# Parked sums of a down projection: added on VectorE at the second part's end, parked from GpSimd's queue, and brought back at spread times

## The chip, the cores and the metric

One core of a Trainium2 chip runs the whole layer in one launch. The time is that of the device for one execution, in microseconds; the median of several runs counts. TensorE (PE in the profile) multiplies matrices, VectorE (DVE) and ScalarE (ACT) work element by element, GpSimd (POOL) and SyncE (SP) issue DMAs here, each in the order of its own list of instructions.

## The reference

An encoder layer for 256 positions of width 2048, in float32. The part that matters here is the channel sub-layer, a gated feed-forward network of width 5632 between two normalisations, whose result is added to the residual stream; the sub-layer behind it needs that sum.

```python
h = h + rms_norm(mixed, g_mix_post[i])
fn = rms_norm(h, g_ffn_pre[i])
ff = (jax.nn.silu(fn @ w_ffn_gate[i]) * (fn @ w_ffn_up[i])) @ w_ffn_down[i]
h = h + rms_norm(ff, g_ffn_post[i])
gate = jax.nn.sigmoid(rms_norm(h, g_ple_pre[i]) @ w_ple_gate[i])
```

## The kernel before

**Products.** Every weight matrix comes from memory in tiles of 256 rows by 512 columns (512 KB, names `wr`, `third`, `lower`, `ple`). ScalarE casts a tile to a high part (`wh`, L624), VectorE takes the remainder (`wl`, L637), and PE does three products for each block (L671 to L673): a tile is 12 matmuls of 128x512. Some of the pairs of tiles in the feed-forward network are multiplied by a scheme with seven products instead of eight (L682 to L684); sums of weight blocks for it are made on VectorE (L572 to L582) and by accumulating DMAs of 256 KB from POOL's queue (L593). There are `W_BUFS = 4` pairs of buffers for split tiles and one more in the space of the gain vector (`w`, in the tile tagged `gain`).

**Stages.** The feed-forward width is worked off in three parts (`PARTS`, 4 + 4 + 3 groups of 512 columns). Each part first makes its columns of gate and up, turns the result (`mid`, moved to `mT` by sixteen small DMAs each) and then multiplies it by its rows of `w_ffn_down`, for four chunks of 512 output columns, two at a time. The chunks of parts 0 and 1 are only partial sums. `down_post` copies them on ScalarE from PSUM to a `mid` tile (L1802) and parks them in DRAM, `parts[0]` and `parts[1]`, from SP's queue (L1805, 512 KB each, eight in all). In part 2, `Sub.chunk` with `add=True` adds the last partial sum to the parked ones in the tiles `mg` (L1472), squares, multiplies by the gain, and the normalisation follows.

**What stands elsewhere meanwhile.** SBUF is short, so the tiles of `h` and `mg` (two of 1 MB each) hold other things during parts 0 to 2. `lower_tile` puts weight tiles of the seven-product scheme into the space of `h0` (slots 0 and 1) and of `mg0` (slots 3 and 4); slot 2 is in `ple`. `sums` lies in the space of `h1`, `s` in that of `mg1`. `h` itself is spilled to DRAM (`spill_h`). After the last product that reads those sums (`two_products`, `i == last_two`) everything comes back: `mg` plainly from `parts[0]` on SP's queue (L1827), then `parts[1]` onto it by accumulating DMAs of 1 MB from POOL's queue (`reload_sums`, `added`, L593), and `h` from its spill (`reload_h`, L1610). The gain vector comes by `next_gain` (L1424).

**Order.** A planner (`Plan`) in the program holds a clock for each engine and a list of generators, each of which says what it will do next, on which engine, at what cost and from when. It picks what can start first and so writes the order of each engine's instructions at build time. A due time given to `plan.add` only sets a place in that order; on the chip an instruction runs when its engine comes to it and its semaphores allow.

Of the kernel before, what the change touches and what calls it, by code (L numbers as in the profile page):

```python
# [10 lines left out]
F32 = mybir.dt.float32  # L11
F32R = mybir.dt.float32r
AF = mybir.ActivationFunctionType
ALU = mybir.AluOpType
AX = mybir.AxisListType

P = 128
S = 256
NT = S // P
D = 2048  # L20
# [7 lines left out]
N = 512  # L28
# [11 lines left out]
RING = 5  # L40
# [37 lines left out]
class Event:  # L78


    t = None
# [134 lines left out]
COST = {"act": 0.15, "dve": 0.08, "move": 150 / 340.0, "landing": 1.7}  # L216


def act(n, tables=COPY, take=None, give=None):
    return ("act", COST["act"] + 0.00082 * n, tables, take, give)  # L220


def dve(n, take=None, give=None):
    return ("dve", COST["dve"] + 0.00104 * n, None, take, give)
# [6 lines left out]
def dma(kb, take=None):  # L231
    return ("dma", kb / 340.0, None, take, None)
# [3 lines left out]
def layer(ctx: ExitStack, tc: tile.TileContext, a: dict, out: bass.AP):  # L236
    nc = tc.nc
# [4 lines left out]
    plan = Plan(wr=R_BUFS, w=W_BUFS, sm=SM_BUFS, acc=4, ev=1, mid=2, bt=2, m2=1, mt=1, sq=1, T0=1, T1=1, T4=1, **{f"{s}{j}": n for s, m, n in (("p", 5, 1), ("t", 3, 0)) for j in range(m)}, wr0=1, w0=1)  # L242

    def f32(t):
        return t.bitcast(F32)
# [11 lines left out]
    lower = {}  # L257
    more_w = {}

    def w_kind(i):  # L260
        return f"w{more_w[i]}" if i in more_w else "w"
# [16 lines left out]
    def raw_kind(i):  # L278
        if i in lower:
            return f"p{lower[i]}"  # L280
        return f"wr{more_raws[i]}" if i in more_raws else "wr"
# [85 lines left out]
    def done(event):  # L367
        event.t = plan.now
# [11 lines left out]
    class Act:  # L380


        def __init__(self, blocks=KD):
            self.at = {}
            self.ev = [Event() for _ in range(blocks)]
            self.sums, self.ev_sums = {}, {}
# [26 lines left out]
    tiles = []  # L413
    segs = []
# [92 lines left out]
    fours = {}  # L507
# [5 lines left out]
    ev_ple = Event()  # L513
# [3 lines left out]
    def pieces(i):  # L517

        return [slice(0, 1), slice(1, 2)] if i < EARLY else [slice(0, 2)]
# [71 lines left out]
    def added(dst, src, ev):  # L591
        yield ("pool", COST["move"], None, None, None)
        nc.gpsimd.dma_start(dst, src, accum_op=ALU.add)  # L593
        plan.now += ADDED
        done(ev)

    def last_sum(i):
        late, last, j, js, _, _ = fours[i]
        b = (3, 6, 7)[j]
        there = Event()  # L600
        yield from added(blocks()[:, b, :], late[:, 0, :], there)
        yield there
        if j == js[-1]:
            raws[last] = blocks()[:, 3:7:3, :] if len(js) == 2 else blocks()[:, 7:8, :]
            done(ev_raw[last, 2])
# [21 lines left out]
    def lo_stream():  # L627
        last_one = max(f[1] for f in fours.values())
        for i in range(len(tiles)):
            at_lo[0] = i  # L630
            for j in pieces(i):
                n = j.stop - j.start
                yield ev_hi[i, j.stop]
                src = raws[i] if n == 2 else raws[i][:, j, :]
                m = slice(j.start, j.start + src.shape[1])
                yield dve(src.shape[1] * N, give=gives.get(i) or raw_kind(i) if j.stop == 2 else None)
                nc.vector.tensor_tensor(  # L637
                    out=los[i][:, m, :], in0=src, in1=f32(his[i][:, m, :]), op=ALU.subtract
                )
                done(ev_lo[i, j.stop])  # L640
            raws.pop(i)
            if i == half_end:
                plan.add(reload_half(), plan.now + 76.0)
            if i in fours:
                plan.add(last_sum(i), plan.now, -2 * SOON)
            if i == last_one:
                done(ev_ple)

    MM = 0.216
    MM4 = 0.86  # L650
# [35 lines left out]
    def spent(i):  # L686
        his.pop(i), los.pop(i)
        at_pe[0] = max(at_pe[0], i)
        free_w(i)
        plan.run()  # L690

    def block(lhs, kx, t):
        return [x[:, t * P : (t + 1) * P] for x in lhs.at[kx]]
# [49 lines left out]
    def two_products(group, j, i):  # L743
        (C1, _, _), (C2, _, _) = group.chunks
        kx = group.sevens[j][1]
        s = group.lhs.sums[kx]
        plan.main(0, ev_lo[i, 2], group.lhs.ev[kx + 1], group.made)
        product(C1.accs[0], block(group.lhs, kx + 1, 0), i, 0, seeded=True)
        product(C2.accs[0], s["S4"], i, 1, seeded=True)
        spent(i)  # L750
        if i == last_two:
            for t in range(NT):
                plan.add(reload_sums(0, t), plan.clk["pe"] + 9.0 + 4.0 * t)
                plan.add(reload_sums(1, t), plan.clk["pe"] + 28.0 + 5.0 * t)
                plan.add(reload_h(t), plan.clk["pe"] + 50.0 + 12.0 * t)

    def one_product(group, js, i):
        (C1, _, _), _ = group.chunks
# [42 lines left out]
    def free_w(i):  # L801
        if i not in keep:
            plan.free[w_kind(i)].append(plan.clk["pe"])
        if i == max(more_w):
            plan.add(next_gain(("ffn", "g_ffn_post"), plan.clk["pe"] + 37.0), plan.clk["pe"] + 37.0)

    keep = set()
    def run_seg(s):
# [567 lines left out]
    for n, c in enumerate(ORDER.split()):  # L1376
        (n0, post), half = CHUNKS[c[0]], int(c[1])
        ch = Chunk(post(half), (open_p1, second_tiles)[n] if n < 2 else None)
# [10 lines left out]
    t2 = {}  # L1389

    class Halves:
        def __init__(self, pool, n):
            self.tiles = [
                pool.tile([P, D], F32, tag=f"{n}{t}", name=f"{n}{t}") for t in range(NT)
            ]

# [48 lines left out]
    ev_sums_back = Event()  # L1445
# [120 lines left out]
    def turn_h(c, hi, lo, nxt, gname):  # L1566
# [10 lines left out]
        for b in range(4):  # L1577
# [7 lines left out]
    spill = ctx.enter_context(  # L1585
        tc.tile_pool(name="spill", bufs=1, space=bass.MemoryType.DRAM)
    ).tile([NT, P, D], F32, name="h_spill")
    parts = [
        ctx.enter_context(
            tc.tile_pool(name=f"parts{i}", bufs=1, space=bass.MemoryType.DRAM)  # L1590
        ).tile([NT, P, D], F32, name=f"part{i}")
        for i in range(2)
    ]
    ev_spilled, ev_back = Event(), Event()
# [6 lines left out]
            nc.sync.dma_start(spill[t], t2["h"].tiles[t])  # L1601
        done(ev_spilled)

    halves_back = []

    def reload_h(t):
        if "back" not in t2:
            t2["back"] = Halves(t2["pool"], "h")
        yield dma(1024)
        nc.sync.dma_start(t2["back"].tiles[t], spill[t])  # L1610
        halves_back.append(t)
        if len(halves_back) == NT:
            t2["h"] = t2["back"]
            done(ev_back)

    half_spill = ctx.enter_context(
        tc.tile_pool(name="half_spill", bufs=1, space=bass.MemoryType.DRAM)
    ).tile([P, NT, D // 2], F32, name="ple_spill")
# [10 lines left out]
    def reload_half():  # L1629
        yield dma(1024)  # L1630
        nc.sync.dma_start(t2["ple"][:, :, 0 : D // 2], half_spill)
        done(ev_half_back)

    def next_gain(g, ready):
        yield from load_gain(g[1])
        done(ev_gain[g[0]])
# [32 lines left out]
    hF = Act()  # L1669
# [9 lines left out]
    def after_mix():  # L1679
# [5 lines left out]
    ch = [  # L1685
        Chunk(sub_post(mix, c, after=after_mix), None if c else open_p2,
              slot="sm" if c == 2 else "acc")
        for c in range(4)
    ]
# [10 lines left out]
    ffn = Sub("ffn", "g_ffn_post", "g_ple_pre")  # L1700
# [17 lines left out]
    def mid_tile():  # L1718
        return t2["pool"].tile([P, NT, N], F32, tag="mid", name="mid", bufs=2)
# [74 lines left out]

    def down_post(part, c):
        def post(ch):
            e = None
            for t in range(NT):
                yield act(N, take=None if t else "mid")
                if not t:  # L1800
                    e = mid_tile()
                nc.scalar.copy(e[:, t, :], ch.accs[t])  # L1802
            ch.release()
            yield dma(512)
            nc.sync.dma_start(  # L1805
                parts[part].rearrange("t p d -> p t d")[:, :, c * N : (c + 1) * N], e
            )
            plan.now += COST["landing"]
            plan.free["mid"].append(plan.now)
            ev_parts.append((part, c))  # L1810
        return post

    ev_parts = []

    def reload_sums(part, t):
        assert len(ev_parts) == 8
        if "mg_back" not in t2:
            t2["mg_back"] = t2["mg"] = Halves(t2["pool"], "mg")
        if part:
            there = Event()  # L1820
            yield from added(t2["mg"].tiles[t], parts[part][t], there)
            yield there
            if t == NT - 1:
                done(ev_sums_back)
        else:
            yield dma(1024)
            nc.sync.dma_start(t2["mg"].tiles[t], parts[0][t])  # L1827

    def after_ffn():
        return next_norm(ffn, hP, rstd_p, ev_rp, ("ple", "g_ple_post"))  # L1830
# [20 lines left out]
    for part, (f0, f1) in enumerate(PARTS):  # L1851
        mid = Mid(f"mid{part}")
        last_part = part == len(PARTS) - 1
        for f in range(f0, f1):
            slot = ring()
            g = Chunk(gate_post(f), slot=slot)
# [191 lines left out]
    n = 0  # L2048
# [6 lines left out]
        if i % (W_BUFS + MORE_W) < MORE_W:  # L2055
            more_w[i] = i % (W_BUFS + MORE_W)
    for n, i in enumerate(sorted(lower)):
        lower[i] = (3, 4, 0, 1, 2)[n % RING]
    first_slot = {i: n % 2 for n, i in enumerate(sorted(fours))}
    for i, (_, last, _, js, _, two) in fours.items():  # L2060
        ev_load[i], ev_load[i + 1] = Event(), Event()
# [1 line left out]
        gives[last] = tuple(f"t{j}" for j in js)  # L2063
    twos = [(j, i) for f, g, j, i in (s for s in segs if s[0] is two_products)]
    last_two = max(i for _, i in twos)
    half_end = max(f[1] for f in fours.values())
    i0 = segs[-1][-1]
    keep.update(range(i0, i0 + 8))
# [120 lines left out]
```

## Time and profile before

| | |
|---|---|
| runs | 1162.78 to 1164.9 us, median 1163.18 us of 3 |
| the profiled execution | 1162.47 us |
| its span, first to last instruction | 1160.7 us |
| PE busy | 1146.8 us (99%), 5219 matmuls |
| DVE, ACT, POOL busy | 887.0 us (76%), 710.5 us (61%), 124.7 us (11%) |
| moved by DMA | 265.86 MB, mean 229 GB/s |

A busy PE is not PE at its peak: the ends of its matmuls are modelled, and a stop shorter than that can hide in them. What it lost is read from the distances between the starts of matmuls. Idle time of another engine is in brackets behind an instruction, with what ended it. "SPq" and "POOLq" are DMA issues of these queues; when the data landed is shown apart from that.

### The profile page before, as it was taken

How to read it: one execution, taken by the hardware profiler on the slowest of the kernel's cores; microseconds unless marked ns; L12 is line 12 of the kernel's file. 1: busy time of each engine (PE TensorE's matmuls, PEld its weight loads, DVE VectorE, ACT ScalarE, POOL GpSimd, SP SyncE). 2: the span in 40 equal slices, each digit the busy share in tenths (PEclk: the TensorE clock that was granted, in tenths of full speed). 3: DMA queues.
4: the chain of work that ended last, by engine and by line, in shares of the span. 5: the costliest groups of instructions: out<-in, count | busy, mean ns of one | idle time of the engine just before them, and what ended most of it. 6: DMA issues, size and time to landing. Idle time of an engine off the chain costs nothing.

```text
span 1160.7 us, 15071 instructions
## 1 busy us (share of the span) xinstructions
PE 1146.8 (99%) x5219; PEld 951.5 (82%) x5219; DVE 887.0 (76%) x1107; ACT 710.5 (61%) x946; POOL 124.7 (11%) x202
## 2 busy tenths in 40 slices
PE   9999999999999999999999999999999999999997
PEld 8888888888888878888888888888888888777786
DVE  6678787888468878988778898988777985368565
ACT  6777777875556545655556566565565654256664
POOL 0000000000000023031000213312000321200000
PEclk9999999999999999999999999999999999999999
DMA  8867566545686987877876786778787677985771
GB/s 307 301 185 232 175 181 207 176 151 198 218 294 191 308 238 250 249 216 215 283 238 229 244 246 203 233 239 248 218 296 236 199 224 245 268 286 195 216 249 73
DMA packets 112732, 265.86 MB, mean 229 GB/s; under 512 B 39184, under 2 KB 46096, under 8 KB 110992
## 3 DMA queue, kind: packets, MB, share of 16 engines
q1 hardware_dynamic: 101744, 247.76, 63.2%
q0 software_dynamic: 10480, 16.79, 8.6%
q8 instruction: 41, 0.67, 0.2%
q10 hardware_dynamic: 432, 0.35, 0.1%
q14 instruction: 35, 0.29, 0.1%
HBM read 247.03 MB, written 9.44 MB: 221 GB/s over the span
## 4 chain that ended last, share of the span: by engine, by line
PE 88%; DMA 5%; DVE 3%; ACT 2%; issue 1%; POOL 1%; SPq 0%; ACTq 0%; DVEq 0%; POOLq 0%
PE acc L673 23%; PE acc L672 23%; PE acc L671 23%; PE acc L684 5%; PE acc L682 5%; PE acc L683 5%; DMA mT<-mid 2%; DMA wr<-in_w_ffn_down 1%; DMA wr<-in_w_ple_gate 1%; DVE wl L637 1%; ACT wh L624 1%; PE tr L326 1%; POOL mT L345 1%; PE warm L2098 0%; PE pg L357 0%
## 5 line engine op out<-in xcount | busy, mean ns | idle before, releaser
L637 DVE TENSOR_TENSOR wl<-wr,wh 128x1024 fp32r<-128x1024 f32 (+1 forms) x313 | 374.7, 1210 | 142.0 <-ACT wh L624 137.5
L624 ACT CAST wh<-wr 128x1024 fp32r<-128x1024 f32 (+1 forms) x313 | 324.7, 1043 | 213.0 <-PE acc L672 134.8
L672 PE MATMUL acc<-wh,hT_mix_lo 128*128 128x512 f32 x400 | 155.9, 390 | 0.3 <-DVE hT_mix_lo L315 0.3
L671 PE MATMUL acc<-wh,hT_mix_hi 128*128 128x512 f32 x400 | 156.0, 390 | 0.0
L673 PE MATMUL acc<-wl,hT_mix_hi 128*128 128x512 f32 x400 | 155.7, 389 | 0.0
L345 POOL DMA_DIRECT2D mT<-mid x152 | 89.0, 596 | 563.1 <-ACT wh L624 401.7
L673 PE MATMUL acc<-wl,hT_hi 128*128 128x512 f32 x320 | 124.6, 390 | 0.0
L671 PE MATMUL acc<-wh,hT_hi 128*128 128x512 f32 x316 | 124.5, 394 | 0.0
L672 PE MATMUL acc<-wh,hT_lo 128*128 128x512 f32 x316 | 123.2, 390 | 0.0
L624 ACT CAST wh<-ple 128x1024 fp32r<-128x1024 f32 (+1 forms) x54 | 53.4, 989 | 68.0 <-DVE ple L576 34.4
L672 PEld LDWEIGHTS acc<-wh,hT_mix_lo 128*128 128x128 f32 x400 | 75.1, 188 | 16.4 <-DVE hT_mix_lo L315 1.0
L671 PEld LDWEIGHTS acc<-wh,hT_mix_hi 128*128 128x128 f32 x400 | 75.1, 188 | 15.5
L673 PEld LDWEIGHTS acc<-wl,hT_mix_hi 128*128 128x128 f32 x400 | 75.1, 188 | 15.5
L637 DVE TENSOR_TENSOR wl<-ple,wh 128x1024 fp32r<-128x1024 f32 (+1 forms) x54 | 61.5, 1142 | 12.7 <-ACT wh L624 12.2
L673 PEld LDWEIGHTS acc<-wl,hT_hi 128*128 128x128 f32 x320 | 60.3, 188 | 12.9
L672 PEld LDWEIGHTS acc<-wh,hT_lo 128*128 128x128 f32 x316 | 59.4, 188 | 11.5
L671 PEld LDWEIGHTS acc<-wh,hT_hi 128*128 128x128 f32 x316 | 59.5, 188 | 11.4
L593 POOL DMA_DIRECT2D ple<-in_w_ffn_up x27 | 24.0, 891 | 234.7 <-DVE wl L637 195.9
L671 PE MATMUL acc<-wh,hT_ffn_hi 128*128 128x512 f32 x104 | 40.9, 393 | 0.8 <-ACT hT_ffn_hi L313 0.8
L672 PE MATMUL acc<-wh,hT_ffn_lo 128*128 128x512 f32 x104 | 40.8, 393 | 0.5 <-DVE hT_ffn_lo L315 0.5
L673 PE MATMUL acc<-wl,hT_ffn_hi 128*128 128x512 f32 x104 | 40.5, 390 | 0.0
L671 PE MATMUL acc<-wh,mid2h 128*128 128x512 f32 x96 | 38.3, 399 | 2.2 <-ACT wh L624 2.2
(431 smaller groups left out, 2422.6 us busy)
## 6 DMA issues: line engine op xcount, KB each, us to landing
wr<-in_w_ffn_gate SPq DMA_DIRECT2D x78, 512.0 KB, 5.4
wr<-in_w_in SPq DMA_DIRECT2D x77, 512.0 KB, 4.6
wr<-in_w_ffn_down SPq DMA_DIRECT2D x65, 512.0 KB, 5.5
wr<-in_w_ffn_up SPq DMA_DIRECT2D x49, 512.0 KB, 5.1
wr<-in_w_out SPq DMA_DIRECT2D x32, 512.0 KB, 4.4
wr<-in_w_ple_gate SPq DMA_DIRECT2D x32, 512.0 KB, 4.6
lower<-in_w_ffn_up SPq DMA_DIRECT2D x22, 512.0 KB, 6.0
ple<-in_w_ffn_up POOLq DMA_DIRECT2D x27, 256.0 KB, 4.3
```

The lines of the kernel that those rows point to most:

```text
L326: nc.tensor.transpose(tr[:, b, t * P : (t + 1) * P], e[:, t, sl], ident)
L345: (nc.gpsimd if i in pool else nc.sync).dma_start(dst[32 * j : 32 * j + 32, :, :, i, :], src[32 * i : 32 * i + 32, :, :, j, :],)
L593: nc.gpsimd.dma_start(dst, src, accum_op=ALU.add)
L624: nc.scalar.copy(his[i][:, 0 : src.shape[1], :] if n == 2 else his[i][:, j, :], src)
L637: nc.vector.tensor_tensor(out=los[i][:, m, :], in0=src, in1=f32(his[i][:, m, :]), op=ALU.subtract)
L671: nc.tensor.matmul(accs[t], hi[:, sl], his[i][:, j, :], start=st, stop=False, **group)
L672: nc.tensor.matmul(accs[t], lo[:, sl], his[i][:, j, :], start=False, stop=False, **group)
L673: nc.tensor.matmul(accs[t], hi[:, sl], los[i][:, j, :], start=False, stop=sp, **group)
L682: nc.tensor.matmul(dst, x[0], wh, start=start, stop=False, skip_group_check=seeded)
L683: nc.tensor.matmul(dst, x[1], wh, start=False, stop=False, skip_group_check=seeded)
L684: nc.tensor.matmul(dst, x[0], wl, start=False, stop=stop, skip_group_check=seeded)
```

## The change

At the end of part 1, `down_post` now loads the parked chunk of part 0 into the `mid` tile from POOL's queue (L1791 of the kernel after), adds the new chunk to it on VectorE (L1798) and parks the sum in `parts[1]`. All parks go out on POOL's queue (L1808). So one parked sum is left, and the accumulating loads of 1 MB are gone. The four tiles come back one by one by `reload` (L1821): `mg0` as soon as the last weight tile in its space is used up (`mg0_end`), `h1` 40 us of planned time after the last use of `sums` (`h1_end`), `mg1` and `h0` 10 and 22 us after `last_two`. The last two weight tiles that would use `mg0`'s space go to slots 0 and 1. The gain's load is due 37 us earlier.

```diff
@@ lo_stream
+            if i == mg0_end:
+                plan.add(reload("mg", 0), plan.now)
+            if i == h1_end:
+                plan.add(reload("h", 1), plan.now + 40.0)
...
@@ two_products
         if i == last_two:
-            for t in range(NT):
-                plan.add(reload_sums(0, t), plan.clk["pe"] + 9.0 + 4.0 * t)
-                plan.add(reload_sums(1, t), plan.clk["pe"] + 28.0 + 5.0 * t)
-                plan.add(reload_h(t), plan.clk["pe"] + 50.0 + 12.0 * t)
+            plan.add(reload("mg", 1), plan.clk["pe"] + 10.0)
+            plan.add(reload("h", 0), plan.clk["pe"] + 22.0)
@@ free_w
         if i == max(more_w):
-            plan.add(next_gain(("ffn", "g_ffn_post"), plan.clk["pe"] + 37.0), plan.clk["pe"] + 37.0)
+            plan.add(next_gain(("ffn", "g_ffn_post"), plan.clk["pe"]), plan.clk["pe"])
@@ down_post
-            e = None
+            sl = slice(c * N, (c + 1) * N)
+            if part:
+                yield ("pool", COST["move"], None, "mid", None)
+                e, here = mid_tile(), Event()
+                nc.gpsimd.dma_start(e, parts[0].rearrange("t p d -> p t d")[:, :, sl])
+                plan.now += COST["landing"]
+                done(here)
+                yield here
             for t in range(NT):
-                yield act(N, take=None if t else "mid")
-                if not t:
-                    e = mid_tile()
-                nc.scalar.copy(e[:, t, :], ch.accs[t])
+                if part:
+                    yield dve(N)
+                    nc.vector.tensor_tensor(
+                        out=e[:, t, :], in0=ch.accs[t], in1=e[:, t, :], op=ALU.add
+                    )
+                else:
+                    yield act(N, take=None if t else "mid")
+                    if not t:
+                        e = mid_tile()
+                    nc.scalar.copy(e[:, t, :], ch.accs[t])
             ch.release()
-            yield dma(512)
-            nc.sync.dma_start(
-                parts[part].rearrange("t p d -> p t d")[:, :, c * N : (c + 1) * N], e
-            )
+            yield ("pool", COST["move"], None, None, None)
+            nc.gpsimd.dma_start(parts[part].rearrange("t p d -> p t d")[:, :, sl], e)
...
-    def reload_sums(part, t):
...
+    def reload(n, t):
+        assert n == "h" or len(ev_parts) == 8
+        yield dma(1024)
+        if (n, t) not in back:
+            back[n, t] = t2["pool"].tile([P, D], F32, tag=f"{n}{t}", name=f"{n}{t}")
+        nc.sync.dma_start(back[n, t], (spill if n == "h" else parts[1])[t])
+        if len([k for k in back if k[0] == n]) == NT:
+            t2[n] = Halves(None, n, [back[n, k] for k in range(NT)])
+            done(ev_back if n == "h" else ev_sums_back)
...
-        lower[i] = (3, 4, 0, 1, 2)[n % RING]
+        lower[i] = (3, 4, 0, 1, 2)[n % RING] if n < len(lower) - 2 else n + 2 - len(lower)
...
+    mg0_end = max(fours[i - 1][5] for i in lower if lower[i] > 2)
+    h1_end = max(i for f, g, j, i in (s for s in segs if s[0] is two_products) if g.lhs is not hF)
```

The order of PE's instructions is the same in both kernels, apart from buffer numbers. Three places on the others:

SP's list in part 2, from the last tile of `w_ffn_up` on, before (`mg` and `h` are the tiles that come back, with buffer numbers; `part_98` is `parts[0]`, `part_101` is `parts[1]`):

```order
L532 DMA wr<-in_w_ffn_up 128x1024
L532 DMA wr<-in_w_ffn_down 128x1024 x3
L1827 DMA mg_8134<-part_98 128x2048
L532 DMA wr<-in_w_ffn_down 128x1024 x2
L1827 DMA mg_8135<-part_98 128x2048
L532 DMA wr<-in_w_ffn_down 128x1024 x2
L345 DMA mT<-mid 32x8x32 x8
L532 DMA wr<-in_w_ffn_down 128x1024 x4
L1424 DMA gain_g_ffn_post<-in_g_ffn_post 128x2048
L532 DMA wr<-in_w_ffn_down 128x1024 x7
L1610 DMA h_8136<-h_spill 128x2048
```

and now:

```order
L1426 DMA gain_g_ffn_post<-in_g_ffn_post 128x2048
L532 DMA wr<-in_w_ffn_up 128x1024
L532 DMA wr<-in_w_ffn_down 128x1024 x3
L1821 DMA mg_8217<-part_101 128x2048
L532 DMA wr<-in_w_ffn_down 128x1024 x4
L345 DMA mT<-mid 32x8x32 x8
L532 DMA wr<-in_w_ffn_down 128x1024 x4
L1821 DMA h_8388<-h_spill 128x2048
L532 DMA wr<-in_w_ffn_down 128x1024 x13
```

One load of `mg` instead of two stands there, the gain has moved ahead of the stage's last tile of `w_ffn_up`, and one half of `h` stands where the gain stood. The other halves have moved up in SP's list, into the gates of part 2, where only weight tiles stood:

```order
L532 DMA lower<-in_w_ffn_up 128x1024
L532 DMA wr<-in_w_ffn_gate 128x1024
L1821 DMA h_7435<-h_spill 128x2048
L532 DMA third<-in_w_ffn_up 128x1024
L532 DMA wr<-in_w_ffn_gate 128x1024
```

```order
L532 DMA wr<-in_w_ffn_gate 128x1024
L532 DMA third<-in_w_ffn_up 128x1024
L1821 DMA mg_7699<-part_101 128x2048
L532 DMA wr<-in_w_ffn_gate 128x1024
L532 DMA lower<-in_w_ffn_up 128x1024
```

The tiles around them are in their old order; the last row of the second piece is one of the two whose slot is another.

POOL's list around the end of part 1, before:

```order
L345 DMA mT<-mid 32x8x32 x8
L593 DMA ple<-in_w_ffn_down 128x512 x3
L593 DMA ple<-in_w_ffn_up 128x512 x6
L345 DMA mT<-mid 32x8x32 x16
L593 DMA ple<-in_w_ffn_up 128x512 x3
```

and now:

```order
L345 DMA mT<-mid 32x8x32 x8
L593 DMA ple<-in_w_ffn_down 128x512 x3
L1791 DMA mid<-part_98 128x2x512 x2
L1808 DMA part_101<-mid 128x2x512 x2
L593 DMA ple<-in_w_ffn_up 128x512 x3
L1791 DMA mid<-part_98 128x2x512 x2
L1808 DMA part_101<-mid 128x2x512 x2
L593 DMA ple<-in_w_ffn_up 128x512 x3
L345 DMA mT<-mid 32x8x32 x16
```

Two loads and two parks stand ahead of each set of three accumulations. On DVE, the adds of the first two chunks stand between the splits of weight tiles, now:

```order
L637 TENSOR_TENSOR wl<-third,wh 128x1024
L1798 TENSOR_TENSOR mid<-acc_6523,mid 128x512
L1798 TENSOR_TENSOR mid<-acc_6524,mid 128x512
L637 TENSOR_TENSOR wl<-wr,wh 128x1024
L1798 TENSOR_TENSOR mid<-acc_6525,mid 128x512
L1798 TENSOR_TENSOR mid<-acc_6526,mid 128x512
L637 TENSOR_TENSOR wl<-lower,wh 128x1024
L637 TENSOR_TENSOR wl<-ple,wh 128x1024
```

Before, the four rows of L637 followed each other there.

More of the change, by code (lines that the diff above doesn't have):

```diff
@@ L641, in lo_stream @@
             raws.pop(i)
+            if i == last_one:
+                done(ev_ple)
+            if i == mg0_end:
+                plan.add(reload("mg", 0), plan.now)
+            if i == h1_end:
+                plan.add(reload("h", 1), plan.now + 40.0)
             if i == half_end:
@@ L645, in lo_stream @@
                 plan.add(last_sum(i), plan.now, -2 * SOON)
-            if i == last_one:
-                done(ev_ple)
     MM = 0.216
@@ L1391, in layer, with __init__ @@
     class Halves:
-        def __init__(self, pool, n):
-            self.tiles = [
+        def __init__(self, pool, n, tiles=None):
+            self.tiles = tiles or [
                 pool.tile([P, D], F32, tag=f"{n}{t}", name=f"{n}{t}") for t in range(NT)
@@ L1602, in spill_h @@
         done(ev_spilled)
[L1604 to L1614, printed above, removed]
     half_spill = ctx.enter_context(
@@ L1811, in down_post @@
         return post
-    ev_parts = []
-    def reload_sums(part, t):
[L1816 to L1827, printed above, removed]
+    ev_parts, back = [], {}
+    def reload(n, t):
[7 more added lines that the diff above has]
+            done(ev_back if n == "h" else ev_sums_back)
     def after_ffn():
```

## The prediction

> **What bounds the kernel now.** The page first: the profiled execution took 1162.47 us, of which the span is
>
> ```profile
> span 1160.7 us, 15071 instructions
> ```
>
> TensorE is the bound. What an edit can win is therefore only time in which its matmuls stand still or run slowly. The list of waits for PE gives the few places where they stand still; after 860 us it has four entries, one pair at one place:
>
> ```profile
> PE acc L671 <- ACT wh L624: 2.2, 2, 1.2
> PE acc L671 <- ACT hT_ffn_hi L313: 0.8, 1, 0.8
> PE acc L672 <- DVE hT_ffn_lo L315: 0.5, 1, 0.5
> ```
>
> The first is in the down projection of the third part. The timeline of PE (start, length, and in brackets the idle time before it with its releaser):
>
> ```profile
> 984.83 0.39 PE L671 MATMUL acc<-wh,mid2h 128*128 128x512 f32 x1
> ...
> 1009.08 0.39 PE L673 MATMUL acc<-wl,mid2h 128*128 128x512 f32 x1
> 1010.51 0.50 PE L671 MATMUL acc<-wh,mid2h 128*128 128x512 f32 x1 [1.05 <-ACT wh L624]
> ...
> 1015.50 0.50 PE L671 MATMUL acc<-wh,mid2h 128*128 128x512 f32 x1 [1.16 <-ACT wh L624]
> ...
> 1018.36 0.63 PE L672 MATMUL acc<-wh,mid2l 128*128 128x512 f32 x1
> ...
> 1021.20 0.40 PE L673 MATMUL acc<-wl,mid2h 128*128 128x512 f32 x1
> ```
>
> From 984.83 to 1009.08 there are 107 steps from one matmul to the next, 24.25 / 107 = 0.2266 us each. From 1009.08 to 1021.20 there are 27, which should take 6.12 us and take 12.12. **So 6.0 us are lost here**: two stops, and after them matmuls of 0.63 us instead of 0.39.
>
> Why it stops is in the chain that ended last, read in this stretch:
>
> ```profile
> 997.25 17.06 DMA wr<-in_w_ffn_down
> ...
> 1014.41 1.05 ACT wh L624
> ```
>
> A weight tile asked for at 997.25 landed 17.06 us later; the cast (ACT), the remainder (DVE) and PE followed it. The DMA issues (KB each, median us to landing) show that such a tile normally takes a third of that, and what is slow:
>
> ```profile
> wr<-in_w_ffn_down SPq DMA_DIRECT2D x65, 512.0 KB, 5.5
> ...
> ple<-in_w_ffn_up POOLq DMA_DIRECT2D x27, 256.0 KB, 4.3
> ...
> part<-mid SPq DMA_DIRECT2D x8, 512.0 KB, 4.9
> ...
> mg<-part SPq DMA_DIRECT2D x2, 1024.0 KB, 8.4
> mg<-part POOLq DMA_DIRECT2D x2, 1024.0 KB, 14.8
> h<-h_spill SPq DMA_DIRECT2D x2, 1024.0 KB, 7.2
> ...
> gain_g_ffn_post<-in_g_ffn_post SPq DMA_DIRECT2D x1, 1024.0 KB, 20.1
> ```
>
> What was sent just before, from the timelines of SP and POOL:
>
> ```profile
> 976.63 0.43 SPq L1827 DMA_DIRECT2D mg<-part  x1
> 978.98 3.85 SPq L532 DMA_DIRECT2D wr<-in_w_ffn_down  x2
> 985.10 5.17 SPq L345 DMA_DIRECT2D mT<-mid  x8
> 990.37 2.53 SPq L532 DMA_DIRECT2D wr<-in_w_ffn_down  x4
> 992.96 0.66 SPq L1424 DMA_DIRECT2D gain_g_ffn_post<-in_g_ffn_post  x1
> ```
> ```profile
> 990.87 1.89 POOL L593 DMA_DIRECT2D mg<-part  x2
> ```
>
> Within 3 us there go out four weight tiles (2 MB), the two accumulating loads (2 MB) and the gain (1 MB). The windows (the last three columns are clock, busy share of the DMA engines, GB/s):
>
> ```profile
> 990.00:996.00 6.00, 6.00 (x28) 4.95 (x28) 2.53 (x4) 3.15 (x4) 2.76 (x4) 1.00 0.92 218
> 996.00:1002.00 6.00, 6.00 (x28) 4.99 (x27) 2.45 (x2) 1.05 (x1) 0.00 (x0) 1.00 1.00 242
> 1002.00:1008.00 6.00, 6.00 (x28) 4.95 (x28) 1.23 (x1) 1.05 (x1) 0.00 (x0) 1.00 1.05 255
> 1008.00:1014.00 6.00, 4.43 (x19) 2.99 (x17) 1.22 (x1) 1.04 (x1) 0.00 (x0) 1.00 0.99 404
> ```
>
> The DMA engines are as full at 996 as at 1008, but move 242 against 404 GB/s; the accumulating loads, issued at 990.87, fill the slow stretch (14.8 us).
>
> [...]
>
> **The change part by part.**
>
> *The accumulating loads go, the rest is spread.* Between 990 and 998 there remain the four weight tiles, half of h (1 MB, right behind them) and the tile that was asked for at 997.25: 3.15 MB ahead of it, and its own 0.52. At the slowest of the four rates, 218 GB/s, it lands 3.67 / 0.218 = 16.8 us after 990.37, at 1007.2; at 404 GB/s after 9.1, at 999.5. The matmul of 1009.08 ends a pass over one tile; without stops another tile follows (12 matmuls, 2.72 us) and then this one, at 1009.31 + 2.72 = 1012.03. It needs it on chip 1.05 + 1.23 us earlier (cast, and the remainder, whose row stands below), by 1009.7. Both bounds are earlier, the worse by 2.5 us. I take the full 6.0 us off. The matmuls of 0.63 us come after the stops and go with them.
>
> *The other loads stand at new places.* The windows there:
>
> ```profile
> 871.00:877.00 6.00, 6.00 (x28) 4.95 (x28) 4.50 (x6) 3.01 (x4) 0.00 (x0) 1.00 0.56 221
> 877.00:883.00 6.00, 6.00 (x28) 4.99 (x27) 5.21 (x6) 3.73 (x4) 0.88 (x1) 1.00 0.19 25
> ...
> 906.00:912.00 6.00, 6.00 (x28) 4.99 (x27) 5.97 (x7) 3.04 (x4) 1.86 (x4) 1.00 0.11 39
> ...
> 960.00:966.00 6.00, 6.00 (x28) 4.97 (x27) 2.42 (x2) 2.67 (x3) 1.30 (x3) 1.00 0.43 109
> ```
>
> SP issues in order and as soon as its waits allow, so the place in its list decides, not the planner's due time. Going by the weight tiles around it, half of h comes to stand after 871, half of mg after 906 (DVE has then released the slot), the gain at 962 once PE has released its buffer. In these stretches the DMA engines are mostly idle (shares 0.56 and 0.19, 0.11, 0.43); 1 MB needs 7.2 to 8.4 us by its rows. Queued behind each on SP are weight tiles; their cover is the lead of the splits, worked out below. The fourth, the other half of mg, stands where one stood before. Price 0; bounds 0 and 8.4 − 5.9 = 2.5 us for each place.
>
> *The adds at the end of the second part.* Eight VectorE adds replace eight ScalarE copies. Their price is that of the same form in the same kernel, and their place is between these rows (DVE timeline; brackets: idle before):
>
> ```profile
> L1472 DVE TENSOR_TENSOR mg<-acc,mg x8: 678/683/692, 1019.1 to 1053.7; 128x512 f32<-128x512 f32 x8
> ```
> ```profile
> 826.11 1.23 DVE L637 TENSOR_TENSOR wl<-third,wh 128x1024 fp32r<-128x1024 f32 x1 [0.22 <-ACT wh L624]
> 828.17 1.23 DVE L637 TENSOR_TENSOR wl<-wr,wh 128x1024 fp32r<-128x1024 f32 x1 [0.83 <-ACT wh L624]
> 830.89 1.22 DVE L637 TENSOR_TENSOR wl<-lower,wh 128x1024 fp32r<-128x1024 f32 x1 [1.49 <-ACT wh L624]
> ...
> 839.05 1.23 DVE L637 TENSOR_TENSOR wl<-wr,wh 128x1024 fp32r<-128x1024 f32 x1 [0.62 <-ACT wh L624]
> ```
>
> Four adds are 4 x 0.683 = 2.73 us; the idle times there are 0.83 + 1.49 + 0.62 = 2.94. So DVE is back on its old times at 839. What it delays in between is covered by the lead: with four split buffers the cast of a tile starts when PE has ended the tile four before; three passes of 2.72 us remain, less 1.05 and 1.23, that is 5.9 us, and for products of six matmuls half the passes, 1.8 us. The second pair of ends has the same pattern. Price 0 (bounds 0 and 1 us in all: 2.73 less the 1.8 of lead).
>
> *The loads of the first part's sums.* They go out on POOL behind the last accumulation and do not wait for PE:
>
> ```profile
> 811.67 0.87 POOL L593 DMA_DIRECT2D ple<-in_w_ffn_down  x1 [7.79 <-DVE wl L637]
> 838.72 0.87 POOL L593 DMA_DIRECT2D ple<-in_w_ffn_up  x1 [26.19 <-DVE wl L637]
> ```
>
> POOL is free from 812.5 and they are wanted when DVE is done with the tile of 826.11, at 827.3: 14.8 us. No row shows a plain 512 KB load from POOL; the nearest are 4.3 us (half the size, accumulating) and 4.9 (same size, from SP), the farthest 14.8 (twice the size, accumulating, in the bunch). I take 4.9, the same size; all three are in time, the last of them just. What stands behind the waiting parks on POOL is the accumulation of 838.72, which is due after the adds.
>
> *Parks on POOL instead of SP*: eight issues leave a queue that nobody was waiting for; 0. *Two ring slots* for the last two tiles: they are reused sooner, but after their release; 0.
>
> **Sum.** 1162.47 − 6.0 = 1156.5 us for the profiled execution. The median of the runs shown, 1163.18, lies 0.7 above it, so the forecast for the median is **1157.2 us**; its own range, from the spread of the runs (0.4 below, 1.7 above the median) is 1156.8 to 1158.9.
>
> **The rivals.**
> A. *Half the stop stays.* The four tiles still queue behind the eight mT issues at 985.10 and go out together with 1 MB behind them. If the tile of 997.25 still needs its 17 us, the stop at 1015.50 remains, about half of the 6.0: 1160.2. For it: the bunch of weight tiles is unchanged. Against: 16.8 us from 990.37, not from 997.25, is the worst rate. Chance 0.09.
> B. *The adds wait for POOL's loads: slower.* Place: DVE at 827, with all splits behind the blocked add. It decides from a landing of 14.8 us on; beyond it each us is a us of PE once the lead (1.8 to 5.9) is used up, at both pairs of ends. From 14.8 + 5.9 + 3.0 = 23.7 us the gain is gone; at 29.6 us, twice the longest POOL row, it costs 2 x (14.8 − 5.9) = 17.8: 1175. For it: the DMA engines are busy there. Against: the longest median of POOL's rows is 14.8, in the bunch that goes. Chance 0.05. [...]
> C. *The bunch only moves.* If two of the four moved loads each hold a weight tile back by 2.5 us, 5.0 come back: 1162.2, no change. For it: no row shows these loads there. Against: shares of 0.11 to 0.56. Chance 0.07.
> D. *More goes.* Were the waits of the next norm (0.8 + 0.5 us) due to late data, they would go too: 1155.9. Against: their releasers are ACT and DVE. Chance 0.05.
>
> **How the numbers follow.** Forecast 0.74, A 0.09, B 0.05, C 0.07, D 0.05. A measurement of this kernel can tell about 0.2% (2.3 us) from no change. Faster than 1160.85: 0.74 + 0.05 + most of A (0.07) = 0.86. Same: C and the rest of A, 0.09. Slower: B, 0.05. The range reaches from 1155.2 (D, less the spread of runs) to 1160.6 (A, with it).
>
> **What would show it.** Right: no PE wait on wh between 1000 and 1025 and a step of 0.2266 throughout; that weight tile landing in under 10 us; no DVE idle time in front of the adds that a DMA ends; half of h landing by 880. Wrong: a wait of DVE on mid<-part (B), a wait of ACT on a weight tile after 871, 906 or 962 (C), or the same tile landing after 1010 (A).

## The result, and the profile after

| | before | after |
|---|---|---|
| median of 12 runs of each on one chip | 1164.72 us (1162.27 to 1168.89) | 1159.68 us (1155.25 to 1162.42) |
| ratio | | 0.9955, 95% interval 0.9941 to 0.9969 |
| the profiled execution | 1162.47 us | 1162.0 us |
| its span | 1160.7 us | 1160.2 us |

The kernel is faster by 0.45% (0.31 to 0.59%); the medians lie 5.0 us apart. The forecast was 1157.2 us and 6.0 us less than before: the time is inside the range, but 2.5 us above the forecast and above the likeliest case's own range (1156.8 to 1158.9). The two profiled executions differ by 0.5 us only, so the first question is where the rest of the gain is in that trace.

The list of waits for PE in the kernel after (engine, line, what it waited for: us in all, times, longest):

```profile
PE acc L686 <- ACT wh L624: 1.5, 1, 1.5
PE acc L688 <- DVE wl L637: 1.5, 2, 0.8
...
PE acc L675 <- ACT hT_ffn_hi L313: 1.0, 1, 1.0
PE acc L676 <- DVE hT_ffn_lo L315: 0.5, 1, 0.5
```

The wait of 2.2 us of the plain products (there L671, here L675) on the cast `wh` is gone. The first row is new, and the second has grown: the profile before has one such wait of 0.7 us (there L684). Both are not in the third part but in the seven-product scheme (L686, L688), long before anything that the change touched. The windows of the stretch that the prediction showed (the last three columns are clock, busy share of the DMA engines, GB/s):

```profile
996.00:1002.00 6.00, 6.00 (x28) 4.99 (x27) 3.65 (x4) 3.41 (x5) 0.00 (x0) 1.00 0.94 319
1002.00:1008.00 6.00, 6.00 (x29) 4.95 (x28) 3.11 (x4) 2.48 (x3) 0.00 (x0) 1.00 1.00 402
1008.00:1014.00 6.00, 6.00 (x28) 4.99 (x27) 3.01 (x3) 2.11 (x2) 0.00 (x0) 1.00 0.72 232
...
1009.00:1021.00 12.00, 12.00 (x55) 9.93 (x54) 7.07 (x9) 6.46 (x10) 0.00 (x0) 1.00 0.60 189
```

The DMA engines, when full, now move 402 GB/s instead of 242 to 255, are no longer full after 1008, and PE starts 28 or 29 matmuls in each 6 us. Three marks in the order of PE, which is the same in both kernels, show the rest: the matmuls numbered 1990, 4530 and 4700 of the kernel before. In the timeline of PE before:

```profile
423.75 0.39 PE L673 MATMUL acc<-w,hT_mix_hi 128*128 128x512 f32 x1
...
1000.69 0.39 PE L672 MATMUL acc<-wh,mid2l 128*128 128x512 f32 x1
...
1045.24 0.39 PE L671 MATMUL acc<-wh,mid2h 128*128 128x512 f32 x1
```

and the same matmuls after:

```profile
426.26 0.39 PE L677 MATMUL acc<-w,hT_mix_hi 128*128 128x512 f32 x1
...
1005.92 0.39 PE L676 MATMUL acc<-wh,mid2l 128*128 128x512 f32 x1
...
1044.46 0.39 PE L675 MATMUL acc<-wh,mid2h 128*128 128x512 f32 x1
```

The last stretch takes 1045.24 − 1000.69 = 44.55 us before and 38.54 after: **6.0 us gone**, as forecast. The middle one, which holds the parks, the adds and the moved loads, takes 576.94 before and 579.66 after, and the first 423.75 and 426.26: there this execution lost 2.7 and 2.5 us. Where in the middle stretch, the windows show, first before, then after (columns: us, PE, PE's weight loads, DVE, ACT, POOL busy, then as above):

```profile
426.00:432.00 6.00, 5.27 (x23) 3.80 (x22) 5.93 (x9) 5.65 (x6) 0.95 (x1) 1.00 0.40 66
```
```profile
426.00:432.00 6.00, 4.10 (x17) 2.74 (x15) 4.29 (x7) 3.13 (x4) 0.00 (x0) 1.00 0.08 31
432.00:438.00 6.00, 4.85 (x20) 3.70 (x21) 5.93 (x8) 4.86 (x6) 0.93 (x1) 1.00 0.52 129
```

At 426 the order on every engine is the same in both kernels, and the first changed instruction (a park) comes after 560. Whether this second stop belongs to one execution or to most is a question for the experiments.

### The profile page after: what moved, and what is told of

The parts are those of the page before. It is cut to its first block, busy times and chain, and to the rows that moved or that the text cites. A ratio compares the mean times of both kernels' runs of the same rounds, so it can differ in the third digit from the quotient of the medians.

```text
span 1160.2 us, 15087 instructions
## 1 busy us (share of the span) xinstructions
PE 1146.0 (99%) x5219; PEld 951.1 (82%) x5219; DVE 891.5 (77%) x1115; ACT 707.3 (61%) x938; POOL 131.5 (11%) x212
## 4 chain that ended last, share of the span: by engine, by line
PE 89%; DMA 4%; DVE 2%; ACT 2%; SPq 1%; issue 1%; POOL 0%; ACTq 0%; DVEq 0%; POOLq 0%
PE acc L677 23%; PE acc L676 23%; PE acc L675 23%; PE acc L688 5%; PE acc L686 5%; PE acc L687 5%; DMA mT<-mid 2%; DMA wr<-in_w_ple_gate 1%; DVE wl L637 1%; ACT wh L624 1%; PE tr L326 1%; DMA lower<-in_w_ffn_up 1%; DMA sq<-ev 0%; DMA av<-in_w_rg_i 0%; SPq L345 0%
## 5 line engine op out<-in xcount | busy, mean ns | idle before, releaser
L637 DVE TENSOR_TENSOR wl<-wr,wh 128x1024 fp32r<-128x1024 f32 (+1 forms) x313 | 374.8, 1210 | 135.7 <-ACT wh L624 132.4
L675 PE MATMUL acc<-wh,hT_mix_hi 128*128 128x512 f32 x400 | 155.9, 390 | 0.0
L675 PE MATMUL acc<-wh,hT_hi 128*128 128x512 f32 x316 | 124.4, 394 | 0.0
L675 PEld LDWEIGHTS acc<-wh,hT_mix_hi 128*128 128x128 f32 x400 | 75.1, 188 | 15.5
L637 DVE TENSOR_TENSOR wl<-ple,wh 128x1024 fp32r<-128x1024 f32 (+1 forms) x54 | 61.5, 1143 | 12.0 <-ACT wh L624 11.4
L675 PEld LDWEIGHTS acc<-wh,hT_hi 128*128 128x128 f32 x316 | 59.4, 188 | 11.5
L675 PE MATMUL acc<-wh,hT_ffn_hi 128*128 128x512 f32 x104 | 40.9, 393 | 1.0 <-ACT hT_ffn_hi L313 1.0
L637 DVE TENSOR_TENSOR wl<-third,wh 128x1024 fp32r<-128x1024 f32 x29 | 35.4, 1219 | 5.5 <-ACT wh L624 5.5
```

The costliest lines, as they stand in the source:

```text
L637: nc.vector.tensor_tensor(out=los[i][:, m, :], in0=src, in1=f32(his[i][:, m, :]), op=ALU.subtract)
L675: nc.tensor.matmul(accs[t], hi[:, sl], his[i][:, j, :], start=st, stop=False, **group)
```

## The experiments

Every kernel was profiled once and timed beside the kernel before (5 to 12 runs each); ratios are to that kernel. The three stretches are those of the marks above, in the profiled execution (every trace holds the same 5219 matmuls in the same order, so a mark is the same matmul in each).

| kernel | median us | ratio, 95% | to mark 1 | mark 1 to 2 | mark 2 to 3 |
|---|---|---|---|---|---|
| before | 1164.72 to 1166.07 | 1 | 423.75 | 576.94 | 44.55 |
| after, the profile above | 1159.68 | 0.9955 (0.9941 to 0.9969) | 426.26 | 579.66 | 38.54 |
| after again | 1159.49 | 0.9959 (0.9945 to 0.9972) | 424.84 | 581.71 | 38.53 |
| plain loads from POOL | 1160.33 | 0.9958 (0.9943 to 0.9973) | 422.96 | 581.65 | 38.53 |
| after, loads late | 1159.81 | 0.9956 (0.9940 to 0.9972) | 422.82 | 580.57 | 38.53 |
| after, accumulating loads back | 1164.20 | 0.9993 (0.9981 to 1.0005) | 422.58 | 581.61 | 43.33 |
| after, loads of the adds late | 1160.94 | 0.9969 (0.9954 to 0.9984) | 423.32 | 582.02 | 38.53 |
| after, parks on SP | 1159.77 | 0.9959 (0.9944 to 0.9975) | 423.41 | 580.54 | 38.54 |
| after, split 8 us later | 1154.98 | 0.9917 (0.9899 to 0.9934) | 423.24 | 575.73 | 38.53 |
| after, split 12 us later | 1154.98 | 0.9915 (0.9899 to 0.9931) | 423.07 | 575.74 | 38.53 |
| before, split 8 us later | 1160.55 | 0.9961 (0.9946 to 0.9976) | 422.42 | 575.74 | 44.54 |
| after, third time | 1159.35 | 0.9953 (0.9937 to 0.9970) | 423.08 | 580.45 | 38.53 |
| after, split 8 us later, again | 1155.28 | 0.9915 (0.9901 to 0.9929) | 423.62 | 575.73 | 38.53 |

**The changed kernel again.** No edit.

> The changed kernel itself, once more, so that the others of this group have it on the same chip. All theories: about 5 us faster than before (ratio 0.994 to 0.997), no PE wait on wh between 1000 and 1025. If the profiled run of it again loses time in 428 to 434 and before 210, that loss belongs to the code that both kernels share; if not, it was that one execution.

Ratio 0.9959, last stretch 38.53. The second stop is there again, and larger: the middle stretch is 4.8 us longer than in the profiled execution of before. So that loss is not of one execution. The first stretch is again longer than before too, by 1.1 us.

**Is it the accumulating kind, or the bytes?** The kernel before, with one line exchanged. The second loads then overwrite the first, so part 0's sums are missing from the result; the planner's costs stay, and the order of every engine's instructions is the same in both traces.

```diff
-            yield from added(t2["mg"].tiles[t], parts[part][t], there)
+            nc.gpsimd.dma_start(t2["mg"].tiles[t], parts[part][t])
```

> The kernel before, where the two 1 MB loads of the second part's sums from GpSimd's queue write mg plainly and do not accumulate; same bytes, same queue, same places (part 0's sums are left out of the result). Theory 1, the accumulating kind is slow and fills the DMA engines at half the rate (242 against 404 GB/s): the loads land in about 5 to 8 us instead of 14.8, the stop at 1009 to 1021 is gone or under 1 us, 5 to 6 us faster than before. Theory 2, it is the bytes of the bunch, whatever their kind: the stop stays within 1.5 us of its 6.0, no more than 1.5 us faster than before.

The stop is gone; the last stretch is that of the changed kernel. The loads themselves still take longer than the 5 to 8 us expected. From its DMA issues between 990 and 1000:

```profile
mg<-part POOLq DMA_DIRECT2D x2, 1024.0 KB, 9.4
gain_g_ffn_post<-in_g_ffn_post SPq DMA_DIRECT2D x1, 1024.0 KB, 13.2
```

The queue row of GpSimd's DMAs shows why the rest is fast enough. Packets, MB and share of 16 engines between 980 and 1020, first before, then with plain loads:

```profile
q0 software_dynamic: 544, 2.36, 30.2%
```
```profile
q0 software_dynamic: 544, 2.36, 17.6%
```

The same packets and bytes occupy the engines for 12.1 of the 40 us when two of the loads accumulate, and for 7.0 when none does. With the sixteen mT moves in that row taken as equal in both, the whole difference, 5.0 us, is the accumulating loads' (2.1 MB). **Theory 1 holds: what stopped PE is that an accumulating byte cost the DMA engines more here than a plain one (12.1 against 7.0 us for that row); the bytes, the queue and the place are harmless here.** Why an accumulating byte cost more is not shown by any run.

**Did the loads have to be spread?** The changed kernel, with SP's loads where they were:

```diff
-                plan.add(reload("mg", 0), plan.now)
-                plan.add(reload("h", 1), plan.now + 40.0)
...
-            plan.add(reload("mg", 1), plan.clk["pe"] + 10.0)
-            plan.add(reload("h", 0), plan.clk["pe"] + 22.0)
+            for t in range(NT):
+                plan.add(reload("mg", t), plan.clk["pe"] + 9.0 + 4.0 * t)
+                plan.add(reload("h", t), plan.clk["pe"] + 50.0 + 12.0 * t)
```

(the gain due 37 us later again, and the two ring slots as before).

> The changed kernel with its adds on VectorE and its parks on GpSimd's queue, but with both halves of mg and of h and the gain loaded where the kernel before loads them (gain in the bunch at 990, h halves behind it). Only SP's order differs from the changed kernel. Theory 1, the accumulating loads make the stop: within 1 us of the changed kernel. Theory 2, the loads have to be spread as well: a stop of 2 to 4 us comes back between 1009 and 1021, and it is that much slower than the changed kernel.

Same time, same stretch. The gain in the bunch, by the DMA issues between 985 and 1015:

```profile
gain_g_ffn_post<-in_g_ffn_post SPq DMA_DIRECT2D x1, 1024.0 KB, 8.0
```

8.0 us instead of 20.1: it had been held up, and held nobody up. Spreading the loads is worth nothing that can be measured here.

**The other direction.** The changed kernel, plus two accumulating loads onto `mg` at the old place, which add part 0's sums a second time. They are the only difference in the lists of the engines:

```diff
+        yield from added(back["mg", t], parts[0][t], there)
...
+                plan.add(once_more(t), plan.clk["pe"] + 28.0 + 5.0 * t)
```

> The changed kernel with two accumulating 1 MB loads from GpSimd's queue put back where the kernel before issues them (they add part 0's sums to mg a second time, so the result has those doubled); everything else stays spread. Theory 1, the accumulating loads alone make the stop: it comes back, 4 to 6 us, and the time is within 1.5 us of the kernel before. Theory 2, the stop needs the gain and h in the same bunch too: at most 2 us slower than the changed kernel.

The last stretch goes from 38.53 to 43.33: 4.8 of the 6.0 us are back, and the ratio is 0.9993. Its windows, and its issues from 990 to 1000:

```profile
996.00:1002.00 6.00, 6.00 (x28) 4.95 (x27) 2.57 (x4) 2.19 (x3) 0.00 (x0) 1.00 0.97 240
1002.00:1008.00 6.00, 5.98 (x27) 4.62 (x25) 1.03 (x1) 1.05 (x1) 0.00 (x0) 1.00 1.06 259
1008.00:1014.00 6.00, 3.76 (x14) 2.50 (x15) 1.92 (x3) 2.09 (x2) 0.00 (x0) 1.00 0.98 358
```
```profile
mg<-part POOLq DMA_DIRECT2D x2, 1024.0 KB, 13.7
```

240 and 259 GB/s at full share again. Why 1.2 of the 6.0 us stay away is open; the bunch is not quite the old one, as half of `h` stands in it where the gain stood. With the two directions together, each with all else unchanged, the cause is shown and not only argued.

**Rival B on purpose.** The loads of the adds wait for PE's end of the chunk:

```diff
-                yield ("pool", COST["move"], None, "mid", None)
-                e, here = mid_tile(), Event()
+                yield act(1, take="mid")
+                e, here = mid_tile(), Event()
+                nc.scalar.copy(e[:, 1, 0:1], ch.accs[1][:, 0:1])
+                yield ("pool", COST["move"], None, None, None)
                 nc.gpsimd.dma_start(e, parts[0].rearrange("t p d -> p t d")[:, :, sl])
-                plan.now += COST["landing"]
+                plan.now += 0.5
```

(With the landing planned at 0.5 us, the four adds of a pair of chunks follow each other on VectorE.)

> The changed kernel, where the four loads of part 0's chunk each wait for PE's end of the chunk (ScalarE writes one column of the tile first), so that VectorE comes to its adds before the data, with the splits of weight tiles queued behind. This makes rival B happen on purpose. By the prediction's sum a load that lands 9.3 us after its issue (the median of L1791 in the changed kernel) and 0.5 us for the column blocks VectorE 9 to 10 us; less the lead of 5.9 us that is 4 us at each of the two pairs of ends, 8 us slower than the changed kernel; with the short lead of 1.8 us 8 us each, 16 slower. The rival theory, that the lead is longer than worked out (accumulators and split buffers cover all of it): under 2 us slower.

The expected 8 us were a miss: 0.9969, about 1.2 us slower than the changed kernel's 0.9959, and the intervals overlap. That is also what the expectation's own rival (a longer lead, under 2 us) would give, so the trace has to decide. It shows both parts of the loss, in the timeline of DVE and in the waits of PE:

```profile
831.64 2.56 DVE L1800 TENSOR_TENSOR mid<-acc,mid 128x512 f32<-128x512 f32 x4 [4.00 <-DMA mid<-part]
```
```profile
PE acc L688 <- DVE w L637: 0.7, 1, 0.7
```

DVE did stand still for a DMA, 4.0 us, with the splits behind it. Waiting and adding took it 6.5 us, and PE lost 0.9 us there and 0.55 at the second pair: the cover is 5.6 us, near the 5.9 of the prediction and far from the 1.8, so the lead is not longer than worked out. What was mis-sized is the landing, 4.8 us by the median here instead of 9.3. So the rival's mechanism exists; the changed kernel keeps it away by issuing the loads 14 us early.

**The queue of the parks.** `nc.gpsimd.dma_start(parts[part]...)` became `nc.sync.dma_start`.

> The changed kernel with all eight parks on SP's queue, where the kernel before has them. Prediction: the queue of the parks is worth 0: within 1 us of the changed kernel, 4 to 6 us faster than before. Rival: on SP the parks of part 1 wait for VectorE's adds with weight loads queued behind them, and PE waits for weight tiles after 832 and 872: 1 to 3 us slower than the changed kernel.

0.9959, as the changed kernel: which queue parks is worth nothing.

**The stop at 426.** The ACT timeline after shows what it hangs on:

```profile
427.02 1.14 ACT L307 CAST mid0h<-mT 128x512 fp32r<-128x512 f32 x2 [8.45 <-DMA mT<-mid]
429.80 1.04 ACT L624 CAST wh<-ple 128x1024 fp32r<-128x1024 f32 x1 [1.64 <-DVE ple L576]
```

ScalarE waits 8.45 us for the sixteen small transfers of the first turned block; VectorE waits for ScalarE; and the weight sum that PE needs next (`ple`, then its cast) stands behind both in program order. The planner had put the split 3 us after its estimate of the landing; the edit makes that 8 or 12 for this one block:

```diff
-            plan.add(carried(mid, kk0, mT), plan.now + (0.5 if soon else 3.0), -SOON if soon else 0.0)
+            plan.add(carried(mid, kk0, mT), plan.now + (0.5 if soon else 3.0 if kk0 or part else 8.0), -SOON if soon else 0.0)
```

> The changed kernel, where the split of the first turned block (mid0, L307 and L309) is due 8 us after its transfer instead of 3, so that the weight sums L572 to L582 and their casts stand ahead of it on VectorE and ScalarE; nothing moves on SP and POOL. Theory: the PE stop at 426 to 434 (2.8 to 4.4 us in five of the six profiled executions so far, 1.1 in that of the kernel before) comes from VectorE and ScalarE waiting in order for the mT transfers, with the weight sums behind; it falls to under 1.1 us and the time is 2 to 3 us below the changed kernel (about 1157). Rival: the weight tiles themselves land late there; no gain.

> As the one with 8 us, but due 12 us later, so that two more weight splits stand ahead of mid0's. Theory: the same 2 to 3 us below the changed kernel, and less spread between executions, as it rides over mT transfers that land still later. Rival: mT's buffer and the sums of mid0 come free too late for the next group and a new PE wait appears after 440: no gain or slower.

Both give 1154.98 us, a larger gain than the 2 to 3 us expected. The same window with 8 us:

```profile
426.00:432.00 6.00, 6.00 (x28) 4.99 (x27) 5.40 (x9) 4.30 (x6) 0.00 (x0) 1.00 0.81 277
```

Between 8 and 12 us no difference shows. That the runs spread less, as expected of the longer delay, is not clear: six runs lie within 3.2 us (8) and 1.7 (12), six of the changed kernel within 2.4 in one group and 4.2 in another. The last group has the same edit on the kernel before, beside both others:

> The kernel before with only the first turned block's split due 8 us instead of 3 after its transfer; accumulating loads and bunch as they were. Theory: the two stops are independent, so it gains what the same edit gained on the changed kernel, 4 to 5.5 us (ratio 0.995 to 0.9965), the stop at 426 to 434 goes and the one at 1009 to 1021 (shifted earlier) stays with 4 to 6 us. Rival: the gain seen on the changed kernel came mostly from other places that the planner reordered after it; then less than 2.5 us here.

> The changed kernel once more, on the same chip as the other two: 5 to 6 us faster than before, stop at 426 to 434 of 2.8 to 4.4 us.

> The changed kernel with the split due 8 us later, once more, beside the changed kernel on the same chip: 1154 to 1156 us, 4 to 5.5 us below the changed kernel, so that the two edits together give 9 to 11 us against before.

On the kernel before the edit gives 0.9961, and the marks show that the stop at 1009 is untouched by it:

```profile
422.42 0.39 PE L673 MATMUL acc<-w,hT_mix_hi 128*128 128x512 f32 x1
...
998.16 0.39 PE L672 MATMUL acc<-wh,mid2l 128*128 128x512 f32 x1
...
1042.70 0.39 PE L671 MATMUL acc<-wh,mid2h 128*128 128x512 f32 x1
```

44.54 in the last stretch, 575.74 in the middle one. The two stops are independent and their gains add: 0.9961 and 0.9953 give 0.9914, and the two edits together measure 0.9915 (0.9901 to 0.9929), some 10 us below the kernel before and 4.1 below the changed kernel (1159.35 to 1155.28). **That version is the fastest of all.**

## Why the prediction was right, and where it was off

*The accumulating loads: right in cause and size.* The stop was worth 6.0 us in the forecast and is 44.55 − 38.54 = 6.0 in the trace. The bunch as the prediction put it was four weight tiles, two accumulating loads and the gain; the runs say that only the accumulating loads were too much, as the gain can stay where it was. The weight tile asked for right behind the bunch now goes out at 1002.12 and lands 5.7 us later, under the 10 that the prediction named. Rival A (half the stop stays with the bunch of weight tiles) falls: no part of it stayed, in any of the profiles without accumulating loads. In the bunch, 1 MB from POOL's queue lands in 9.4 us by the median when written plainly, and in 13.7 to 16.2 when accumulating.

One reading of the stop was coarse. The prediction counts two stops and matmuls of 0.63 us behind them; PE's timeline has four stops, as each wait for a cast is followed by one of 0.5 us for the remainder (the row `acc L673 <- DVE wl L637: 1.0, 2, 0.5` of its waits). By the distances between starts they are 4.4 of the 6.0 us. The other 1.6 us are the longer matmuls, and these are matmuls at half the clock: the profile before has (PE, weight loads, DVE, ACT, POOL, then granted clock, DMA share, GB/s)

```profile
1009.00:1021.00 12.00, 8.74 (x29) 5.81 (x28) 6.48 (x7) 6.36 (x8) 0.00 (x0) 0.86 0.82 305
...
1018.50:1019.00 0.50, 0.50 (x3) 0.41 (x2) 0.50 (x1) 0.50 (x1) 0.00 (x0) 0.50 0.91 369
```

while the row of 1009 to 1021 after, shown above, has a clock of 1.00.

*The loads at new places: price 0, right.* Their issues after:

```profile
h<-h_spill SPq DMA_DIRECT2D x2, 1024.0 KB, 9.2
mg<-part SPq DMA_DIRECT2D x2, 1024.0 KB, 8.1
...
gain_g_ffn_post<-in_g_ffn_post SPq DMA_DIRECT2D x1, 1024.0 KB, 7.0
```

They land in 7 to 10 us, and no wait of PE between 871 and 996 appears, so rival C falls. That half of `h` would be there by 880 was a shade early: issued at 876.51, which is 871.3 on the clock of before, and landed 10.0 us later.

*Adds, part loads and parks: 0, right, and now to a hundredth.* With the split moved, the middle stretch, which holds all of them, takes 575.74 us in the kernel before and 575.73 in the changed one. In the timelines of POOL and DVE after, no idle time stands before the adds:

```profile
817.72 1.80 POOL L1791 DMA_DIRECT2D mid<-part  x2
```
```profile
832.17 1.28 DVE L1798 TENSOR_TENSOR mid<-acc,mid 128x512 f32<-128x512 f32 x2
833.40 1.22 DVE L637 TENSOR_TENSOR wl<-wr,wh 128x1024 fp32r<-128x1024 f32 x1
834.54 1.28 DVE L1798 TENSOR_TENSOR mid<-acc,mid 128x512 f32<-128x512 f32 x2
```

*A term that was mis-sized without harm:* the loads of part 0's chunks were put at 4.9 us. The issues say

```profile
part<-mid POOLq DMA_DIRECT2D x8, 512.0 KB, 6.9
...
mid<-part POOLq DMA_DIRECT2D x4, 512.0 KB, 9.3
```

nearly twice that, and for the four one by one the view of that line has

```profile
DMA to landing us min/median/max: 8.1/9.3/12.1
```

The first had 832.17 − 817.72 = 14.5 us and landed in 8.1, so it was 6.3 us early, where the sum had thought of 10. The slowest, the last of the four, landed at 871.70, 4.3 us ahead of its add at 876.02. Rival B stayed away, but by less than it seemed.

*The step that failed is the last one,* from the profiled execution to the median: "0.7 above it". In the runs with the changed kernel, before had a median of 1164.72, that is 2.3 above its profiled execution and not 0.7; this is 1.5 of the 2.5 us between 1157.2 and 1159.68. The other 1.0 us lies between the 6.0 us that the traces show and the 5.0 us between the medians, and the interval of the ratio (3.6 to 6.9 us) does not tell these apart. The marks give a likely reason for the 1.5, argued from one trace: that one execution had a middle stretch of 576.94, 1.2 us above the 575.7 without the stop at 426. In the eight other profiled executions with that part of the order it was 3.9 to 6.3 above (some 1.5 us of the longest are the late loads' own). The first stretch, where no kernel has an edit, varies as well, from 422.42 to 426.26. The one trace was of a lucky execution, and the sum took it, with the median of only three runs, for the typical one. The ends of the range do not follow from their parts either: with the spread that the prediction states, D gives 1155.9 − 0.4 = 1155.5 and A 1160.2 + 1.7 = 1161.9, not 1155.2 and 1160.6; the measured time is inside both. Rival D (the waits at 1058 and 1094 go too) did not happen: the rows of `hT_ffn` stand at 1.0 and 0.5.

## What to carry to other kernels

When DMA engines read as full, look at GB/s beside the share: here 242 to 255 GB/s at shares of 1.00 to 1.05, against 402 at 1.00 in the changed kernel, gave away a kind of transfer that cost more per byte, accumulation. An add on an engine with idle time, at a place where the data pass anyway, replaced it here for nothing (575.73 against 575.74 us in the middle stretch). Before a sum is made against one profiled execution, ask which of its waits hang on a DMA landing just in time, since these can vary from run to run, as the stop at 426 did (a middle stretch of 576.94 us in the kernel before, 579.66 to 581.71 in the changed one); the place found so here was worth nearly as much as the change. On two engines that work in the order of their lists, putting what comes from a DMA behind what was already on chip won 4.1 us here (1159.35 to 1155.28).

## What the runs showed of the hardware

The accumulating DMAs cost about twice what plain ones would: taking the mT moves as equal, 2.1 MB cost 5.0 us of all 16 engines more than the same bytes written plainly. What a plain write of them takes alone is seen from the 402 GB/s of the full window after (423 with the plain loads): 2.1 MB / 410 GB/s = 5.1 us, so the factor is 2.0 by this estimate. The changed kernel has the mT moves alone in that queue's row between 980 and 1020:

```profile
q0 software_dynamic: 256, 0.26, 4.4%
```

That is 1.8 of the 40 us. Taken off the 12.1 and the 7.0, it leaves 10.3 us for the accumulating loads and 5.3 for the plain ones, again a factor of about 2.

The stops at 426 cost more than themselves. In the second profile of the changed kernel PE was idle for 2.6 us between 427 and 437, and the granted clock (the third column from the right) was half in the window of 6.5 us behind the longest stop:

```profile
427.00:430.40 3.40, 1.50 (x7) 0.74 (x5) 3.37 (x7) 1.54 (x3) 0.00 (x0) 0.99 0.00 0
430.50:437.00 6.50, 5.78 (x14) 4.42 (x14) 6.43 (x8) 5.29 (x6) 0.93 (x1) 0.50 0.52 113
```

In its first profile 3.05 us of idle time at the same place (the two windows of 426 to 438 above) left the clock at 1.00. The middle stretch took 581.71 in the one and 579.66 in the other, 6.0 and 3.9 us above the 575.73 with the split moved. Of the eight executions that lost 3.9 us or more in that stretch, the first profile is the only one that kept its clock: between 426 and 438 the mean granted clock is 0.72 or 0.86 in six of the seven others, and the seventh, with the loads of the adds late, has 0.996 over its whole span, where the first profile has 0.999. By the starts of matmuls no single stop in the second profile was longer than 2.1 us, and in the kernel before stops of at most 1.3 us, between 1009 and 1017, were followed by the half clock too (0.50 at 1018.5). How long PE has to stand still for that, and why one row of stops is followed by it and another not, is not shown.
